# A long transformer layer on one core: its opening loads and multiplies x's first four feature tiles by token tile, and two weight loads change queue

## The chip, the cores and the metric

The kernel runs on one core of one Trainium2 chip. The metric is the device time of one execution in microseconds (us). The kernel before has a median of 1103.39 us in 3 runs (1103.22 to 1104.03). One execution was also profiled.

## The reference

The reference is one layer on x of 256 tokens by 2048 features, all in float32:

```python
h = rms_norm(x, attn_norm)
p = h @ w_in                      # 2048 x 6152: q, k, v of two groups of 8 heads, forget gates
out_a = forgetting_attention(...) # softmax with a cumulative forget bias
out_b = stick_breaking_attention(...)
x = x + concat(rms_norm(out_a), rms_norm(out_b)) @ w_out
h = rms_norm(x, ffn_norm)
u = causal depthwise conv of width 3 over h @ w_up, plus conv_b
x = x + (silu(gate) * val) @ w_down
```

Only the first steps matter here: the norm's weight on x, and the first 512 columns of the product with w_in (the queries of four heads). The division by the root mean square is a factor of each token and is applied to the finished product.

## The kernel before

**How products are made.** TensorE works in a fast 32-bit format with fewer bits of mantissa, called F32R here, so each factor is split into a high part (a copy into F32R) and a low part (the rest), and each product is three: high by high, low of x by high of w, high of x by low of w. The x side is `hT`: 16 feature tiles of 128 features (k = 0 to 15), each with a high and a low part for 256 tokens, which are two token tiles of 128 (t = 0, 1). The w side is `w_hi` and `w_lo`.

**The work as a whole.** After the opening comes the rest of the projections, the heads of both groups, the output projection and the feed-forward network. Each loads weights on SyncE's queue (SP below), copies the high part on ScalarE (`split`, line 207), subtracts for the low part on VectorE (line 208), and multiplies on TensorE (lines 229, 254, 260 and 1053).

**The opening** (`opening`, lines 385 to 474) makes `acc_q0`, 256 tokens by 512 columns. It goes through the 16 feature tiles in 8 steps c of two tiles each. Its order on TensorE, VectorE, ScalarE and SP is the order in which the code is written (a manual schedule, line 476), so an instruction that waits holds back everything behind it on its engine. The parts:

- `load_x(k, n)` (line 90) brings n feature tiles of x for both token tiles, on SP's queue. `load_w(c, which)` (line 391) brings the 512 columns of w_in for the two feature tiles of step c, or for one of them, on the queue that it is given. A half step of w is 256 KB, and so are two feature tiles of x.
- The norm's weight, 8 KB, is loaded into `prow` on ScalarE's queue (line 434) and transposed by `columns` (line 126) into `ga`, one column for each feature tile. Line 435 loads ScalarE's function table.
- `keep_busy(n)` (line 379) is n multiplications of zeros into an idle PSUM tile.
- `transposed_split(k, ga, n)` (line 133) transposes n feature tiles of x, for both token tiles, into a PSUM tile `ps_x`, one TensorE instruction for each 128 by 128 square (line 138). ScalarE then writes the high part, scaled by `ga` (line 143), and VectorE the low part (line 146). `ps_x` comes from a pool `psb` of two buffers: a third set of transposes waits until the first buffer has been read for the last time.
- `split_w(c)` (line 402) makes the high and low part of w for step c. In steps 0 and 1 most of the high parts are made on VectorE (lines 409 and 415), later all on ScalarE (line 418). The low parts are made on VectorE (line 419).
- `multiply(c, i, n, high)` (line 423) is the products of a step, line 428: both token tiles, first all that use `w_hi`, then all that use `w_lo`. A step has 12 matmuls of 512 columns, the opening 96.
- `sums_of_squares` (line 151) squares 512 features of one token tile on ScalarE, for the norm's factor, which is needed after the opening.

The first eight loads in their order on the two queues, 256 KB each but for the norm's weight:

```
ScalarE  prow (8 KB)    table load     w, tile k=1      w, tile k=2
SP       x, tiles 0, 1  w, tile k=0    x, tiles 2, 3    w, tile k=3    x, tiles 4, 5 ...
```

From the ninth load on, a load is issued when the one eight places ahead of it, counted over both queues, has landed. The products of step 0 are 8 matmuls with `w_hi` for k = 0 and 1, then four transposes (tiles 2 and 3), then 4 matmuls with `w_lo`. Then come the four transposes of tiles 4 and 5, then step 1, and so on: the transposes of step c + 1 stand ahead of the products of step c.

Of the kernel before, what the change touches and what calls it, by code (L numbers as in the profile page):

```python
# [45 lines left out]
def hybrid_layer(  # L46
# [19 lines left out]
    nc = tc.nc  # L66
    act, dve = nc.scalar, nc.vector
    xf = x.rearrange("b s d -> (b s) d")
# [18 lines left out]
    xt = [x2[:, t, :] for t in range(NT)]  # L87
    xp = xf.rearrange("(t p) d -> p t d", p=P)

    def load_x(k, n):  # L90
        nc.sync.dma_start(x2[:, :, k * P : (k + n) * P], xp[:, :, k * P : (k + n) * P])

    ident = cs[:, C_ID : C_ID + P]
# [27 lines left out]
    ga = const.tile([P, KT], F32, name="ga")  # L121
# [9 lines left out]
    hT = big.tile([P, KT, 2, S], F32R, name="hT")  # L131

    def transposed_split(k, g, n=2):

        ps = psb.tile([P, 2, S], F32, name="ps_x", tag="t")
        for j in range(n):
            for t in range(NT):
                nc.tensor.transpose(  # L138
                    ps[:, j, t * P : (t + 1) * P], xt[t][:, (k + j) * P : (k + j + 1) * P], ident
                )  # L140
        for j in range(n):
            i = k + j
            act.activation(hT[:, i, 0, :], ps[:, j, :], AF.Identity, scale=g[:, i : i + 1])
        for j in range(n):
            i = k + j
            dve.scalar_tensor_tensor(
                hT[:, i, 1, :], ps[:, j, :], g[:, i : i + 1], f32(hT[:, i, 0, :]),
                op0=ALU.mult, op1=ALU.subtract,
            )

    def sums_of_squares(ss, c, tiles=range(NT)):

        for t in tiles:
            junk = late.tile([P, 512], F32, name="junk", tag="raw", bufs=4)
            act.activation(junk, xt[t][:, c * 512 : (c + 1) * 512], AF.Square, accum_out=ss[:, t, c : c + 1])
# [78 lines left out]
    def of_half(h, part, t):  # L234
        return h[:, part, t * P : (t + 1) * P]
# [51 lines left out]
    with ExitStack() as actx:  # L287
# [91 lines left out]
        def keep_busy(n):  # L379
            for _ in range(n):  # L380
                nc.tensor.matmul(idle, zeros[:, :P], zeros, start=True, stop=True)

        ss1 = const.tile([P, NT, 4], F32, name="ss1")

        def opening():

            acc = psa.tile([P, NT, 512], F32, name="acc", tag="acc")
            pairs = [[(0, 1), (1, 1)]] + [[(0, 2)]] * 7
            raws, parts = [], []

            def load_w(c, which=None, queue=nc.sync):

                if c == len(raws):
                    raw = wraw.tile([P, 2048], F32, name="w_raw", tag="w_raw")
                    raws.extend([raw[:, :1024], raw[:, 1024:]])
                for i, n in [(which, 1)] if which is not None else [(0, 2)]:
                    queue.dma_start(
                        raws[c][:, i * 512 : (i + n) * 512].rearrange("p (a b) -> p a b", a=n),
                        rows_of(wi, 2 * c + i, n, 0, 512),
                    )  # L400

            def split_w(c):
                hi = whi.tile([P, 2048], F32R, name="w_hi", tag="w_hi")
                lo = wlo.tile([P, 2048], F32R, name="w_lo", tag="w_lo")
                parts.append([t[:, :1024].rearrange("p (a b) -> p a b", a=2) for t in (hi, lo)])
                for i, n in pairs[c]:
                    cols = slice(i * 512, (i + n) * 512)
                    if c == i == 0:
                        dve.tensor_copy(hi[:, cols], raws[c][:, cols])
                        for k in range(2):  # L410
                            transposed_split(k, ga, 1)
                    elif c == 1:
                        for j in range(2):
                            half = slice(512 * j, 512 * (j + 1))
                            dve.tensor_copy(hi[:, half], raws[c][:, half])
                        transposed_split(2, ga)
                    else:
                        act.copy(hi[:, cols], raws[c][:, cols])
                    dve.tensor_tensor(
                        lo[:, cols], raws[c][:, cols], f32(hi[:, cols]), op=ALU.subtract  # L420
                    )

            def multiply(c, i, n, high):
                hi, lo = (p[:, i : i + n] for p in parts[c])
                order = [(j, l, hi) for j in range(n) for l in range(2)] if high else [(j, 0, lo) for j in range(n)]
                for m, (j, l, r) in enumerate(order):
                    for t in range(NT):
                        nc.tensor.matmul(  # L428
                            acc[:, t, :], of_half(hT[:, 2 * c + i + j], l, t), r[:, j, :],
                            start=high and c == i == m == 0, stop=not high and c == 7 and m == n - 1,  # L430
                        )

            load_x(0, 2)
            nc.scalar.dma_start(prow[:KT, :], attn_norm[0].rearrange("(n p) -> n p", p=P))
            act.preload_act_table_set("natural_log_exp_and_others")
# [18 lines left out]
            def behind(c):  # L454
                if c:
                    transposed_split(2 * c + 2, ga)
                split_w(c + 1)

            multiply(0, 0, 1, True)
            multiply(0, 1, 1, True)  # L460
            behind(0)
            sums_of_squares(ss1, 0, [0])
            multiply(0, 0, 1, False)
            multiply(0, 1, 1, False)
            for c in range(1, 8):
                if c < 7:
                    behind(c)
                sums_of_squares(ss1, c // 2, [c % 2])
                if c == 2:
                    load_w(6)  # L470
                    load_w(7)
                multiply(c, 0, 2, True)
                multiply(c, 0, 2, False)
            return acc

        with tc.high_priority(offset=AHEAD), tc.manual_schedule(
# [698 lines left out]
```

## Time and profile before

| what | value |
|---|---|
| median of 3 runs | 1103.39 us |
| lowest, highest | 1103.22, 1104.03 us |
| the profiled execution's own time | 1103.81 us |
| its span, first to last instruction | 1102.0 us |
| granted TensorE clock, mean | 1.000 |
| bytes read from HBM | 242.82 MB |

The profiled execution took 1.8 us more than its span, and 0.42 us more than the median of the runs. PE is TensorE's matmul side, PEld its weight loads, DVE is VectorE, ACT is ScalarE, POOL is GpSimd, SP is SyncE; ACTq and SPq are the instructions with which these two issue DMAs. L428 is line 428 of the kernel. In a view in order of time, the first number is the start and the second the duration, both in us, and a group "x4" is four instructions in a row; where idle time came ahead, a bracket names it and what ended it.

### The profile page before, as it was taken

How to read it: one execution, taken by the hardware profiler on the slowest of the kernel's cores; microseconds unless marked ns; L12 is line 12 of the kernel's file. 1: busy time of each engine (PE TensorE's matmuls, PEld its weight loads, DVE VectorE, ACT ScalarE, POOL GpSimd, SP SyncE). 2: the span in 40 equal slices, each digit the busy share in tenths (PEclk: the TensorE clock that was granted, in tenths of full speed). 3: DMA queues.
4: the chain of work that ended last, by engine and by line, in shares of the span. 5: the costliest groups of instructions: out<-in, count | busy, mean ns of one | idle time of the engine just before them, and what ended most of it. 6: DMA issues, size and time to landing. Idle time of an engine off the chain costs nothing.

```text
span 1102.0 us, 14826 instructions
## 1 busy us (share of the span) xinstructions
PE 1096.5 (99%) x5868; PEld 951.2 (86%) x5868; DVE 877.7 (80%) x941; ACT 701.9 (64%) x879; POOL 44.4 (4%) x46
## 2 busy tenths in 40 slices
PE   9999999999999999999999999999999999999998
PEld 7998888888888888888888888888888888888887
DVE  5655777975775677689889988889798889889896
ACT  6544556664653566677767776767676777677753
POOL 0000000000000000000000010100000010100010
PEclk9999999999999999999999999999999999999999
DMA  8776654576545396558989597986979689997985
GB/s 288 171 244 230 188 156 153 153 231 197 184 161 186 112 317 196 181 191 209 288 223 312 191 234 264 261 269 177 315 209 303 217 218 282 241 266 198 322 208 177
DMA packets 179407, 245.89 MB, mean 223 GB/s; under 512 B 4432, under 2 KB 119018, under 8 KB 179082
## 3 DMA queue, kind: packets, MB, share of 16 engines
q1 hardware_dynamic: 162458, 209.67, 58.6%
q0 software_dynamic: 16560, 34.75, 16.8%
q8 instruction: 46, 0.75, 0.3%
q10 hardware_dynamic: 320, 0.53, 0.1%
q14 instruction: 23, 0.19, 0.0%
HBM read 242.82 MB, written 2.11 MB: 222 GB/s over the span
## 4 chain that ended last, share of the span: by engine, by line
PE 99%; DMA 0%; DVE 0%; SPq 0%; issue 0%
PE pu L254 34%; PE acc L229 22%; PE pu L260 18%; PE bank_a L229 10%; PE bank_b L229 5%; PE bank_c L229 2%; PE acc L428 2%; PE acc L1053 1%; PE ps_x L138 1%; PE ps_o L593 1%; PE bank_a L1053 1%; PE ps_p L607 0%; DMA w_raw<-in_w_in_dram 0%; PE ps_o L594 0%; PE ps_h L307 0%; PE ps_s L522 0%
## 5 line engine op out<-in xcount | busy, mean ns | idle before, releaser
L208 DVE TENSOR_TENSOR w_lo<-w_raw,w_hi 128x2048 fp32r<-128x2048 f32 (+1 forms) x196 | 439.6, 2246 | 129.5 <-ACT w_hi L207 128.6
L207 ACT CAST w_hi<-w_raw 128x2048 fp32r<-128x2048 f32 (+1 forms) x196 | 367.3, 1877 | 235.9 <-PE acc L229 66.6
L254 PE MATMUL pu<-hT,w_hi 128*128 128x512 f32 x1664 | 394.0, 390 | 0.0
L254 PEld LDWEIGHTS pu<-hT,w_hi 128*128 128x128 f32 x1664 | 310.3, 188 | 63.2
L260 PEld LDWEIGHTS pu<-hT,w_lo 128*128 128x128 f32 x1664 | 211.9, 191 | 7.0
L260 PE MATMUL pu<-hT,w_lo 128*128 128x256 f32 x1664 | 215.1, 283 | 0.0
L229 PE MATMUL acc<-w_hi,hT 128*128 128x512 f32 (+1 forms) x576 | 124.5, 368 | 0.0
L229 PEld LDWEIGHTS acc<-w_hi,hT 128*128 128x128 f32 x576 | 101.5, 188 | 14.3
L207 ACT CAST w_hi<-w_sum 128x2048 fp32r<-128x2048 f32 x30 | 57.3, 1909 | 44.2 <-PE pu L254 36.6
L208 DVE TENSOR_TENSOR w_lo<-w_sum,w_hi 128x2048 fp32r<-128x2048 f32 x30 | 68.7, 2290 | 20.8 <-ACT w_hi L207 20.7
L870 ACT ACTIVATE tap<-up,ccol 128x256 f32<-128x256 f32 x176 | 74.6, 495 | 0.0
L229 PE MATMUL acc<-w_lo,hT 128*128 128x512 f32 (+1 forms) x288 | 64.6, 366 | 0.0
L229 PEld LDWEIGHTS acc<-w_lo,hT 128*128 128x128 f32 x288 | 51.6, 188 | 7.5
L975 POOL DMA_DIRECT2D w_sum<-in_w_down_dram x20 | 25.7, 1284 | 797.7 <-DVE w_lo L208 786.1
L229 PE MATMUL acc<-w_hi,oT 128*128 128x512 f32 x192 | 46.0, 392 | 0.0
L229 PEld LDWEIGHTS acc<-w_hi,oT 128*128 128x128 f32 x192 | 35.7, 188 | 7.3
L229 PE MATMUL bank_a<-w_hi,g 128*128 128x512 f32 x160 | 40.0, 392 | 0.0
L229 PE MATMUL bank_b<-w_hi,s 128*128 128x512 f32 x160 | 40.0, 392 | 0.0
L229 PE MATMUL bank_a<-w_hi,s 128*128 128x512 f32 x160 | 40.0, 392 | 0.0
L229 PEld LDWEIGHTS bank_b<-w_hi,s 128*128 128x128 f32 x160 | 28.9, 189 | 5.2
L229 PEld LDWEIGHTS bank_a<-w_hi,g 128*128 128x128 f32 x160 | 28.8, 189 | 5.3
L229 PEld LDWEIGHTS bank_a<-w_hi,s 128*128 128x128 f32 x160 | 28.9, 189 | 5.2
(211 smaller groups left out, 1068.7 us busy)
## 6 DMA issues: line engine op xcount, KB each, us to landing
w_raw<-in_w_up_dram SPq DMA_DIRECT2D x88, 1024.0 KB, 7.5
w_raw<-in_w_down_dram SPq DMA_DIRECT2D x44, 1024.0 KB, 6.4
w_raw<-in_w_in_dram SPq DMA_DIRECT2D x36, 1024.0 KB, 5.4
w_sum<-in_w_down_dram POOLq DMA_DIRECT2D x20, 1024.0 KB, 9.9
w_raw<-in_w_out_dram SPq DMA_DIRECT2D x16, 1024.0 KB, 5.1
w_raw<-in_w_down_dram POOLq DMA_DIRECT2D x10, 1024.0 KB, 14.9
w_raw<-in_w_in_dram SPq DMA_DIRECT2D x12, 688.0 KB, 4.2
w_raw<-in_w_in_dram SPq DMA_DIRECT2D x6, 512.0 KB, 6.8
```

Source lines behind the costliest of these rows:

```text
L138: nc.tensor.transpose(ps[:, j, t * P : (t + 1) * P], xt[t][:, (k + j) * P : (k + j + 1) * P], ident)
L207: act.copy(hi[:, :n], raw[:, :n])
L208: dve.tensor_tensor(lo[:, :n], raw[:, :n], f32(hi[:, :n]), op=ALU.subtract)
L229: nc.tensor.matmul(o, lhs(i, l, t), r[:, i, :], start=starts and j == 0, stop=stops and j == 3 * n - 1, skip_group_check=more,)
L254: nc.tensor.matmul(acc[:, j, :], hi[:, i, j * P : (j + 1) * P], hT[:, k].rearrange("p a b -> p (a b)"), start=k == 0, stop=low_first and k ...
L260: nc.tensor.matmul(acc[:, j, S:], lo[:, i, j * P : (j + 1) * P], hT[:, k, 0, :], start=False, stop=not low_first and k == KT - 1,)
L428: nc.tensor.matmul(acc[:, t, :], of_half(hT[:, 2 * c + i + j], l, t), r[:, j, :], start=high and c == i == m == 0, stop=not high and c == ...
L593: nc.tensor.matmul(po, v[j][:, hs], wp[:, k], start=i == 0, stop=False)
L870: act.activation(taps[w][:, j, :], u[:, j, w : w + S], AF.Copy, scale=ccol[:, w, f : f + 1])
L975: nc.gpsimd.dma_start(mem[into][:, : nk * 512].rearrange("p (a b) -> p a b", a=nk), src, accum_op=ALU.add)
L1053: nc.tensor.matmul(o, of_half(g, l, t), r[:, i, c0 : c0 + cols], start=kh == 0 and j == 0, stop=kh == n - 1 and j == 11,)
```

## The change

It touches `opening` alone.

1. The first four feature tiles of x are loaded by token tile: two loads of 128 rows by 512 features, 256 KB each, on SP's queue, in place of `load_x(0, 2)` and `load_x(2, 2)`. The next four come in one load of 512 KB.
2. The weights of k = 0 and k = 1 both go on ScalarE's queue behind the norm's weight, and the table load stands behind these three. The weights of k = 2 and 3 go on SP's queue behind the two loads of x.
3. The four tiles of token tile 0 are transposed together into one `ps_x` (`a`), later those of token tile 1 into another (`b`). Step 0 is multiplied one feature tile and one token tile at a time, high, low of w, low of x: (k, t) = (0, 0), the transposes of token tile 1, (1, 0), (0, 1), (1, 1).
4. High and low parts of x for tiles 0 to 3 are made 128 tokens at a time. The high part of w for k = 0 stays on VectorE; those for k = 1, 2 and 3 are made on ScalarE, where k = 2 and 3 were on VectorE before.
5. The zeros' multiplications go from 14 and 4 to 12, 2 and 3. The sum of squares of token tile 0's first 512 features moves from step 0 to step 4.

The new code, cut:

```diff
+            def load_tile(t):
+                nc.sync.dma_start(xt[t][:, : 4 * P], xf[t * P : (t + 1) * P, : 4 * P])
...
+            def transposed_tile(t):
+                ps = psb.tile([P, 4, P], F32, name="ps_x", tag="t")
+                for k in range(4):
+                    nc.tensor.transpose(ps[:, k, :], xt[t][:, k * P : (k + 1) * P], ident)
+                return ps
...
+            def multiply_one(k, t):
+                hi, lo = (s[:, k % 2, :] for s in parts[k // 2])
+                for m, (l, r) in enumerate(((0, hi), (0, lo), (1, hi))):
+                    nc.tensor.matmul(
+                        acc[:, t, :], of_half(hT[:, k], l, t), r, start=k == m == 0, stop=False
+                    )
...
-            load_x(0, 2)
             nc.scalar.dma_start(prow[:KT, :], attn_norm[0].rearrange("(n p) -> n p", p=P))
+            load_tile(0)
+            load_w(0, 0, nc.scalar)
+            load_tile(1)
+            load_w(0, 1, nc.scalar)
+            load_w(1, 0)
+            load_w(1, 1)
             act.preload_act_table_set("natural_log_exp_and_others")
-            load_w(0, 0)
-            load_w(0, 1, nc.scalar)
-            load_x(2, 2)
-            load_w(1, 0, nc.scalar)
-            load_w(1, 1)
-            load_x(4, 2)
+            load_x(4, 4)
             load_w(2)
-            load_x(6, 2)
             load_w(3)
...
-            keep_busy(14)
+            keep_busy(12)
             columns(ga, prow[:KT, :], KT)
-            split_w(0)
-            keep_busy(4)
+            keep_busy(2)
+            a = transposed_tile(0)
+            keep_busy(3)
+            part_tiles(0)
+            high_part(0, 0, 1, dve.tensor_copy)
+            high_x(a, 0, 0)
+            high_x(a, 0, 1)
+            low_part(0, 0, 1)
+            low_x(a, 0, 0)
+            multiply_one(0, 0)
+            b = transposed_tile(1)
+            high_part(0, 1, 1, act.copy)
+            low_x(a, 0, 1)
+            low_part(0, 1, 1)
+            multiply_one(1, 0)
+            for k in range(2):
+                high_x(b, 1, k)
+                low_x(b, 1, k)
+            multiply_one(0, 1)
+            multiply_one(1, 1)
+            part_tiles(1)
+            for i in range(2):
+                high_x(a, 0, 2 + i)
+                high_part(1, i, 1, act.copy)
+                high_x(b, 1, 2 + i)
+                low_x(a, 0, 2 + i)
+                low_part(1, i, 1)
+                low_x(b, 1, 2 + i)
```

`high_part` copies w's high part on the engine that it is given and `low_part` subtracts on VectorE; `high_x(ps, t, k)` is ScalarE's scaled copy of 128 tokens and `low_x` VectorE's rest. From step 1 on the loop is as before, with the transposes of tiles 4 and 5 ahead of step 1's products.

More of the change, by code (lines that the diff above doesn't have):

```diff
@@ L426, in multiply @@
+            def multiply(c, high):
+                hi, lo = parts[c]
+                order = [(j, l, hi) for j in range(2) for l in range(2)] if high else [(j, 0, lo) for j in range(2)]
                 for m, (j, l, r) in enumerate(order):
@@ L471, in opening @@
                     load_w(7)
-                multiply(c, 0, 2, True)
-                multiply(c, 0, 2, False)
+                multiply(c, True)
+                multiply(c, False)
             return acc
```

62 lines of the change are left out of this document (28 added, 34 removed).

## The prediction

> **What bounds the kernel now.** I read the page first, then a view of the engines' busy time by stretches, then the chain of waits and the instructions in order of time for the opening.
>
> ```profile
> span 1102.0 us, 14826 instructions
> PE 1096.5 (99%) x5868; PEld 951.2 (86%) x5868; DVE 877.7 (80%) x941; ACT 701.9 (64%) x879; POOL 44.4 (4%) x46
> ```
>
> ```profile
> 0.00:6.50 6.50, 4.29 (x23) 2.87 (x23) 0.82 (x4) 2.38 (x4) 1.09 (x8) 1.00 0.68 195
> 6.50:9.80 3.30, 3.21 (x16) 2.70 (x17) 2.61 (x6) 1.03 (x3) 0.00 (x0) 1.00 1.04 366
> 9.80:32.00 22.20, 22.20 (x109) 17.96 (x108) 16.23 (x25) 17.37 (x37) 0.00 (x0) 1.00 0.75 258
> 32.00:560.00 528.00, 528.00 (x2873) 462.01 (x2873) 385.62 (x493) 312.32 (x440) 8.40 (x11) 1.00 0.64 198
> ```
>
> In the second fence each row has the stretch, its length, the busy time (and count) of PE, PEld, DVE, ACT and POOL, the granted clock, the DMA engines' busy share and GB/s. TensorE is busy for all of the 22.20 us from 9.80 on and all of the 528.00 us behind them. There is nothing to hide a delay in and nothing that would swallow a gain: what the opening gains or loses on TensorE before it becomes dense reaches the end in full. So the whole question is one number, the time at which TensorE reaches the first instruction from which both kernels do the same work without a gap. I take the transposes of tiles 4 and 5, at 9.87 us in the kernel before. Both kernels have behind it the same matmuls and transposes, and ahead of it the same 12 products of step 0.
>
> ```profile
> 0.73 0.46 ACTq L434 DMA_DIRECT2D prow<-in_attn_norm_dram  x1
> 0.74 0.43 SPq L91 DMA_DIRECT2D x<-in_x_dram  x1
> 1.22 1.28 ACT L435 ACT_TABLE_LOAD   x1 [1.22 <-PEq L1160]
> 1.23 0.46 SPq L397 DMA_DIRECT2D w_raw<-in_w_in_dram  x1
> 1.25 0.94 ACTq L397 DMA_DIRECT2D w_raw<-in_w_in_dram  x2
> ...
> 4.45 0.66 PE L138 MATMUL ps_x<-cs,x 128*128 128x128 f32 x4 [0.20 <-DMA x<-in_x_dram]
> ...
> 4.93 0.84 ACT L143 ACTIVATE hT<-ps_x,ga 128x256 fp32r<-128x256 f32 x2 [2.42 <-PE ps_x L138]
> ...
> 6.02 0.43 DVE L409 CAST w_hi<-w_raw 128x512 fp32r<-128x512 f32 x1 [1.56 <-DMA w_raw<-in_w_in_dram]
> 6.24 0.62 ACT L418 CAST w_hi<-w_raw 128x512 fp32r<-128x512 f32 x1 [0.48 <-DMA w_raw<-in_w_in_dram]
> 6.37 0.87 DVE L146 SCALAR_TENSOR_TENSOR hT<-ps_x,ga,hT 128x256 fp32r<-128x256 f32 x2
> ...
> 6.59 2.06 PE L428 MATMUL acc<-w_hi,hT 128*128 128x512 f32 x8 [1.05 <-DVE w_hi L409]
> 7.15 1.28 DVE L419 TENSOR_TENSOR w_lo<-w_raw,w_hi 128x512 fp32r<-128x512 f32 x2
> ...
> 8.50 0.60 PE L138 MATMUL ps_x<-cs,x 128*128 128x128 f32 x4
> ...
> 8.85 1.18 PE L428 MATMUL acc<-w_lo,hT 128*128 128x512 f32 x4
> ...
> 9.87 0.60 PE L138 MATMUL ps_x<-cs,x 128*128 128x128 f32 x4
> ```
>
> These are the opening's instructions in order of time. What starts the products is the weight of k = 0, not x: x's first tiles are there at 4.45, and the weight, issued on SP at 1.23, ends VectorE's wait at 6.02. Its copy of 0.43 us and 0.14 us to the matmul give 6.59. From there TensorE has work that is ready: eight matmuls with `w_hi` (8.50 - 6.59, some 0.23 us each with the switch) while VectorE and ScalarE make what follows. The weight of k = 1, first of the two on ScalarE's queue, issued at 1.25, ends a wait at 6.24.
>
> **The change part by part.** No matmul and no transpose is added or removed. Hidden ahead of the first product are four transposes in both kernels; four more stand between the products of step 0 in both. The zeros (one fewer) run while TensorE has nothing else. So the sum is of waits alone.
>
> *The loads.* The weight of k = 0 now is ScalarE's second DMA. It is issued when the prow DMA ends, at 1.25 instead of 1.23: no earlier. It takes the very place that k = 1's weight has before, behind prow on that queue, and beside it SP's queue again carries 256 KB of x and 256 KB more. The nearest row is 6.24, and I take it. The weight of k = 1 then takes the place of ScalarE's third DMA, for which a view of the DMA issues at that moment has the landing:
>
> ```profile
> w_raw<-in_w_in_dram ACTq DMA_DIRECT2D x1, 256.0 KB, 5.9
> ```
>
> It is issued at 1.72 (half of the 0.94 us behind 1.25), so 1.72 + 5.9 = 7.62; before, k = 1 landed at 6.24. Token tile 1 of x takes the place of SP's second load, 6.02. The queues' shares of what moved from 2 to 3 us (first fence) and from 4 to 5 us (second) are
>
> ```profile
> q1 hardware_dynamic: 199, 0.20, 76.2%
> q10 hardware_dynamic: 29, 0.01, 5.3%
> ```
>
> ```profile
> q10 hardware_dynamic: 107, 0.19, 54.7%
> q1 hardware_dynamic: 90, 0.13, 50.4%
> ```
>
> with packets, MB and share; q1 is SP's and q10 ScalarE's. ScalarE's moved 0.01 MB in the first, and took its share only later. [...]
>
> *Step 0 tile by tile.* Durations that the trace doesn't have are those of 128 columns. For ScalarE they lie between half of a 256-column copy (0.84 / 2 / 2 = 0.21) and all of it (0.42); I take 0.30. For VectorE's rest they lie between 0.22 and 0.44 (0.87 / 2); I take 0.28. A 512-column subtraction is 0.64 (1.28 / 2), a 512-column copy 0.43 on VectorE and 0.62 on ScalarE; from an engine's end to TensorE I take 0.14 as above.
>
> 1. k = 0 lands at 6.24, the copy ends at 6.67, the first matmul starts at 6.81.
> 2. The second needs `w_lo` and the third the low part of x, both from VectorE behind that copy: 6.67 + 0.64 + 0.28 = 7.59, third matmul at 7.73, TensorE free at 7.96. From 6.59 on it did six matmuls in this time before ((7.96 - 6.59) / 0.23); here three. The new wait holds the whole queue, the transposes of token tile 1 among it.
> 3. Those four transposes take 0.35 (8.85 - 8.50): 8.31. What waits for them is ScalarE's copies for t = 1.
> 4. (1, 0) needs k = 1's weight: 7.62, copy on ScalarE to 8.24, first matmul 8.38, `w_lo` to 8.88, second matmul 9.02, free behind the third at 9.48.
> 5. Six more matmuls, 0.23 each, with all that they need at hand (ScalarE's two copies of 0.30 end by 8.9, VectorE's rests by 9.5): 10.86.
> 6. The transposes of tiles 4 and 5 also need the first `ps_x` back: it is read for the last time by VectorE's rest of tile 3. Behind 8.24 ScalarE makes three copies of 128 columns (9.14), `w_hi` of k = 2 (9.76); VectorE its `w_lo` (10.40) and two rests (10.96). With 0.14 that is 11.10.
>
> So the point comes at 11.10 instead of 9.87, 1.2 us later. Instructions of one engine that don't wait overlap a little (6.02 + 0.43 is 6.45, the next starts at 6.37: 0.08), which over the last chain's few neighbours is some 0.2. I take **1.0 us later**.
>
> *Behind it.* ScalarE gets the moved sum of squares, in step 4:
>
> ```profile
> 15.41 0.64 ACT L155 ACTIVATE junk<-x 128x512 f32<-128x512 f32 x1
> 15.94 0.20 ACT L155 ACTIVATION_READ_ACCUMULATOR junk<-x 128x1 f32 x1
> 16.94 0.47 ACT L143 ACTIVATE hT<-ps_x,ga 128x256 fp32r<-128x256 f32 x1 [0.81 <-PE ps_x L138]
> ```
>
> 0.64 + 0.20 = 0.84 lie in the 0.81 in which it idles in each step; cost nothing, and without that cover at most 0.84 once. The DMA order behind the first six loads is as before but for x's tiles 4 to 7 in one load; up to and with step 2's weights it is 2.62 MB, and by the stretches 195 GB/s for 6.5 us and 366 GB/s for 3.3 us have moved 2.48 MB by 9.8. Those weights are needed when ScalarE has copied tiles 4 and 5, past 12. Cost nothing.
>
> The sum: 1103.8 (the profiled execution, span 1102.0 and 1.8 around it) + 1.0 = 1104.8; that execution stood 0.4 over the median, so the forecast is **1104.4 us**.
>
> **The rivals.**
>
> *ScalarE's weights come early.* Before, the table load (1.22, 1.28 us) stands ahead of ScalarE's weight DMAs; now behind. If it held them back, k = 0 would land after as long a time as x's first load: issued at 0.74, there at 4.45, so 3.7, hence 1.25 + 3.7 = 4.95, and k = 1 after the 4.8 of SP's weight (6.02 - 1.23), at 6.5. For it: 0.01 MB on q10 from 2 to 3 us, though issued by 1.72. Against it: the DMA issue is recorded at 1.25, inside the table load. Then (1, 0) starts by 6.5 + 0.62 + 0.14 = 7.26, its second matmul at 7.9, TensorE is free at 9.74, and the buffer comes back at 7.12 + 2.86 = 9.98: +0.1, less 0.2 of overlap, and down to -0.8 if both weights come 0.7 earlier still. I price it at -0.3: 1103.1 us. Even here step 6's chain, not the first matmul, sets the gain.
>
> *The clock is lost.* This one ends slower beyond doubt. The zeros of the start show two speeds:
>
> ```profile
> 1.06 3.04 PE L381 MATMUL idle<-zeros 128*128 128x256 bf16 x14 [1.06 <-DVE zeros L371]
> ...
> 4.95 0.60 PE L381 MATMUL idle<-zeros 128*128 128x256 bf16 x4
> ```
>
> 14 in 3.04 us, 0.22 each, and later 4 in 0.60, the last ones 0.11 apart (0.60 less the 0.27 of the last, by three). The fast speed came after some 3 us of dense work. The change has fewer zeros ahead of prow and more gaps between 6.8 and 10. If it runs three of those us at half speed, some nine matmuls and four transposes take 9 x 0.23 + 0.35 = 2.4 us more, of which the waits swallow some 0.9: +1.5, in all +2.5, 1105.9 us. It decides from 1.2 us of lost clock on top of the forecast. Against it: in the kernel before TensorE idles from 5.5 to 6.59 and loses nothing. [...]
>
> *It does not do what it says.* If the tile-by-tile order meets its data as early as before but no earlier, the wait of step 2 and that of step 4 fall into each other and the point stays near 9.9: 1103.4 us. It is the upper end of the first rival, and I count it there.
>
> **How the numbers follow.** Forecast 0.58, weights early (or no effect) 0.32, clock lost 0.10. A measurement of this kernel tells about 0.2%, 2.2 us, from no change: below 1101.2 or above 1105.6. Faster than that would need TensorE's first product some 2 us earlier and none of the new waits: 0.02, of the first rival's far end. Slower than that: most of the clock rival, and the forecast's tail with k = 1 later than 7.62 (it now shares with two SP loads of weights): 0.09. Within 0.2%: 0.89. The range takes the first rival at -0.8 (1102.6) and the forecast with k = 1 landing 1.2 later (1105.6, each us later there being a us).
>
> **What would show it.** In the profile after: VectorE's first copy of w near 6.2 (early rival: 5); ScalarE's copy of k = 1 near 7.6; between the first and second matmul of (0, 0) a wait of some 0.5 put down to VectorE's `w_lo`; the first four transposes of line 138 near 10.9, waiting for VectorE; 22 us without a gap behind them; the zeros behind prow at 0.11 us. Wrong would be a first product before 6, a stop behind the point, or granted clock below 1.00.

## The result and the profile after

| | before | after |
|---|---|---|
| median of the runs side by side | 1103.30 us (6 runs, 1103.10 to 1104.03) | 1107.39 us (6 runs, 1106.45 to 1107.77) |
| the profiled execution's own time | 1103.81 us | 1107.20 us |
| its span | 1102.0 us | 1105.4 us |
| mean granted clock | 1.000 | 0.998 |

The kernel after is slower: a ratio of 1.0035 with a 95% interval of 1.0022 to 1.0048, some 4 us. The forecast was 1104.4 us in a range that ended at 1105.6, most of its chance on no change that can be measured, and 0.09 above 1105.6. It had the direction, with a quarter of the size; and one of its own signs of being wrong came, a granted clock below 1.00.

The page of the kernel after, the two lines to set beside those of before:

```profile
span 1105.4 us, 14829 instructions
PE 1098.6 (99%) x5867; PEld 952.5 (86%) x5867; DVE 878.2 (79%) x944; ACT 703.5 (64%) x885; POOL 44.4 (4%) x46
```

The span has grown by 3.4 us and TensorE's busy time by 2.1, with one instruction fewer. So some of its instructions take longer: the four transposes of token tile 1 have 1.06 us, four transposes before 0.60. The engines' busy time by stretches, of the kernel after, with the columns of the prediction's second fence (behind the five engines come the granted clock, the DMA engines' busy share and GB/s):

```profile
0.00:6.50 6.50, 4.35 (x22) 2.89 (x22) 0.34 (x2) 1.91 (x3) 1.09 (x8) 1.00 0.62 181
6.50:9.80 3.30, 2.21 (x8) 1.67 (x8) 2.33 (x5) 0.62 (x1) 0.00 (x0) 0.79 1.05 398
9.80:14.00 4.20, 3.96 (x16) 3.00 (x16) 3.03 (x8) 3.02 (x9) 0.00 (x0) 0.76 1.04 388
14.00:18.00 4.00, 4.00 (x21) 3.29 (x20) 2.19 (x4) 3.22 (x8) 0.00 (x0) 1.00 1.05 385
32.00:560.00 528.00, 528.00 (x2866) 461.69 (x2866) 385.01 (x494) 313.27 (x444) 8.41 (x11) 1.00 0.63 198
```

From 14 us on TensorE is dense, as it was from 9.8 on before. From 6.5 to 9.8 it has 8 instructions where it had 16, and the clock granted is 0.79 from 6.5 to 9.8 and 0.76 from 9.8 to 14. So the loss lies where the prediction looked for it, ahead of the transposes of tiles 4 and 5, and it arrives in full: these start at 13.16 instead of 9.87, 3.29 later, and the span is 3.4 longer.

The instructions of the kernel after in order of time:

```profile
1.18 0.92 ACTq L396 DMA_DIRECT2D w_raw<-in_w_in_dram  x2
...
6.85 0.43 DVE L410 CAST w_hi<-w_raw 128x512 fp32r<-128x512 f32 x1 [2.15 <-DMA w_raw<-in_w_in_dram]
...
7.43 0.47 PE L444 MATMUL acc<-w_hi,hT 128*128 128x512 f32 x1 [1.58 <-DVE w_hi L410]
...
8.06 0.52 PE L444 MATMUL acc<-w_lo,hT 128*128 128x512 f32 x1 [0.16 <-DVE w_lo L417]
8.41 0.65 PE L444 MATMUL acc<-w_hi,hT 128*128 128x512 f32 x1
8.44 0.62 ACT L410 CAST w_hi<-w_raw 128x512 fp32r<-128x512 f32 x1 [2.25 <-DMA w_raw<-in_w_in_dram]
8.85 1.06 PE L427 MATMUL ps_x<-cs,x 128*128 128x128 f32 x4
...
10.73 0.62 ACT L431 ACTIVATE hT<-ps_x,ga 128x128 fp32r<-128x128 f32 x2 [0.42 <-DVE hT L436]
11.13 0.61 DVE L436 SCALAR_TENSOR_TENSOR hT<-ps_x,ga,hT 128x128 fp32r<-128x128 f32 x2 [0.43 <-ACT hT L431]
...
13.16 0.66 PE L138 MATMUL ps_x<-cs,x 128*128 128x128 f32 x4 [0.23 <-DVE hT L436]
```

Three things differ from the forecast. The weight of k = 0 ends VectorE's wait at 6.85, not 6.24. The four transposes of token tile 1 take 1.06 us; before, four took 0.60. And ScalarE and VectorE wait for each other (the brackets 0.42 and 0.43). The 0.43 was to be expected, since VectorE's low part is made from ScalarE's high part; the 0.42 was not. The chain of waits of the kernel after shows how the last two reach the point; its columns are start, duration, and engine, tile and line:

```profile
8.06 0.99 PE acc L444 x2
9.05 0.87 PE ps_x L427 x4
...
9.95 0.38 ACT hT L431
...
10.35 0.36 DVE hT L436
...
10.73 0.62 ACT hT L431 x2
11.36 0.52 ACT w_hi L410
...
11.90 0.56 DVE w_lo L417
...
12.51 0.61 DVE hT L436 x2
...
13.16 0.66 PE ps_x L138 x4
```

From the end of the transposes of token tile 1 (9.05 + 0.87 = 9.92) to the point at 13.16 the chain doesn't touch TensorE at all. It goes through ScalarE, VectorE, ScalarE, VectorE. The second piece is a turn: ScalarE's second copy out of `b` waits until VectorE has taken the first rest out of the same `b`, though from other columns. It is the PSUM tile that they take turns on and not `hT`, which the brackets name: from 11.13 to 11.35 ScalarE copies out of `a` (the second of its two at 10.73) while VectorE takes a rest out of `b`, and both write `hT`.

The same view by stretches that are one clock window (3.41 us) long, of the kernel after and then of the kernel before:

```profile
5.01:8.43 3.42, 1.68 (x11) 1.01 (x9) 1.54 (x4) 0.63 (x2) 0.00 (x0) 1.00 1.00 367
8.43:11.84 3.41, 3.41 (x11) 2.83 (x11) 1.75 (x5) 2.10 (x6) 0.00 (x0) 0.50 1.04 392
```

```profile
3.83:7.24 3.41, 2.16 (x14) 1.50 (x13) 1.39 (x5) 1.46 (x3) 0.00 (x0) 1.00 0.99 320
```

After 3.42 us in which TensorE was busy for 1.68, 3.41 us were granted at 0.50. In the kernel before a stretch of that length with 2.16 busy is followed by none.

### The profile page after: what moved, and what is told of

It is laid out like the page before. It is cut to its first block, busy times and chain, and to the rows that moved or that the text cites. A ratio compares the mean times of both kernels' runs of the same rounds, so it can differ in the third digit from the quotient of the medians.

```text
span 1105.4 us, 14829 instructions
## 1 busy us (share of the span) xinstructions
PE 1098.6 (99%) x5867; PEld 952.5 (86%) x5867; DVE 878.2 (79%) x944; ACT 703.5 (64%) x885; POOL 44.4 (4%) x46
## 4 chain that ended last, share of the span: by engine, by line
PE 99%; DMA 1%; DVE 0%; ACT 0%; ACTq 0%; issue 0%
PE pu L254 34%; PE acc L229 22%; PE pu L260 18%; PE bank_a L229 10%; PE bank_b L229 5%; PE bank_c L229 2%; PE acc L453 2%; PE acc L1094 1%; PE ps_x L138 1%; PE ps_o L634 1%; DMA w_raw<-in_w_in_dram 1%; PE bank_a L1094 1%; PE ps_p L648 0%; PE ps_o L635 0%; PE ps_h L307 0%; PE ps_s L563 0%
```

## The experiments

Three theories stood at the start; the expectations call them by letters. **M**, mine: three things add up, the weight of k = 0 that comes late, the turns of ScalarE and VectorE on one PSUM tile, and half a clock. **K**: the clock is the whole of it. **W**: it is the waits of TensorE in the new order and for its weights, and the clock plays no part. A difference of single medians below about 1 us is inside the intervals here; such ones are read from the traces, and a trace is one execution: the four kernels with the same loads (after, e1, e8, e11) have the weight of k = 0 at 6.51 to 7.04. "The point" is the start of the transposes of tiles 4 and 5.

| kernel | what it is | k = 0 lands | first product | point | median, us | ratio to before (95%) |
|---|---|---|---|---|---|---|
| before | | 6.02 | 6.59 | 9.87 | 1103.30 to 1103.87 | 1 |
| after | | 6.85 | 7.43 | 13.16 | 1107.39 | 1.0035 (1.0022 to 1.0048) |
| e1_filled | after, zeros in the gaps | 6.76 | 7.77 | 12.76 | 1106.56 | 1.0026 (1.0016 to 1.0035) |
| e4_order | after, weights as before | 5.83 | 6.41 | 12.37 | 1106.45 | 1.0026 (1.0016 to 1.0035) |
| e8_highs | after, no turns | 7.04 | 7.62 | 12.94 | 1106.98 | 1.0030 (1.0017 to 1.0043) |
| e11_highs_filled | e1 and e8 | 6.51 | 7.14 | 11.49 | 1105.70 | 1.0017 (1.0008 to 1.0026) |
| e10_mended | e1, e4 and e8 | 6.00 | 7.38 | 11.38 | 1105.25 | 1.0012 (1.0003 to 1.0022) |
| e6_table | after, table load first | 6.60 | 7.17 | 12.91 | 1107.24 | 1.0031 (1.0020 to 1.0042) |
| e3_queues | before, weights as after | 6.01 | 6.58 | 10.91 | 1105.09 | 1.0013 (1.0004 to 1.0023) |
| e9_tiles | e3, x by token tile | 7.05 | 8.26 | 13.47 | 1106.37 | 1.0030 (1.0017 to 1.0044) |
| e2_thinned | before, fewer zeros | 6.03 | 6.60 | 9.90 | 1104.36 | 1.0009 (1.0000 to 1.0018) |
| e12_before_filled | before, more zeros | 5.91 | 6.48 | 9.78 | 1103.91 | 1.0003 (0.9994 to 1.0012) |
| e7_first | before, x on ScalarE's queue | by 7.22 | 8.24 | 12.87 | 1107.82 | 1.0036 (1.0023 to 1.0049) |
| e13_wfirst | before, weight ahead of prow | by 4.87 | 7.45 | 11.48 | 1105.95 | 1.0021 (1.0012 to 1.0030) |

**e1_filled: the gaps of the kernel after filled with zeros**, so that the clock is kept.

```diff
-            def multiply_one(k, t):
+            def multiply_one(k, t, fill=0):
                 hi, lo = (s[:, k % 2, :] for s in parts[k // 2])
                 for m, (l, r) in enumerate(((0, hi), (0, lo), (1, hi))):
+                    if m == 1:
+                        keep_busy(fill)
...
-            keep_busy(3)
+            keep_busy(15)
...
-            multiply_one(0, 0)
+            multiply_one(0, 0, 3)
...
-            multiply_one(1, 0)
+            multiply_one(1, 0, 3)
```

> The kernel after, with more multiplications of zeros on TensorE: 15 in place of 3 ahead of the first product, and 3 between the first and second matmul of the products (0, 0) and (1, 0). Nothing else changes; its loads and waits are those of the kernel after. Theory M (late weights, then a serial chain of ScalarE and VectorE, and one clock window of 3.4 us lost on top): the clock stays at full speed, the matmuls between 8.4 and 11.8 us take 0.23 us in place of 0.43, but the chain of ScalarE and VectorE holds the transposes of tiles 4 and 5 (13.16 us in the kernel after) at about 12.5, so about 0.7 us faster than the kernel after: 1106.7. Theory K (the clock is the whole of what the forecast missed): 1.7 us faster, 1105.7, transposes near 11.5. Theory W (the waits alone, the clock's loss lies inside them): no change, 1107.4.

1106.56 us, as M said. In order of time:

```profile
5.38 2.63 PE L381 MATMUL idle<-zeros 128*128 128x256 bf16 x15
7.77 0.48 PE L446 MATMUL acc<-w_hi,hT 128*128 128x512 f32 x1
...
8.90 0.60 PE L427 MATMUL ps_x<-cs,x 128*128 128x128 f32 x4
...
12.76 0.66 PE L138 MATMUL ps_x<-cs,x 128*128 128x128 f32 x4 [0.83 <-DVE hT L436]
```

The transposes take 0.60 again, so the clock was kept, and all ten runs have a mean clock of 1.000, where four of the kernel after's six have 0.998. The fifteen zeros have a price: in this execution they ran at half speed until 7.08 (the fifteen took 2.63 us; in the kernel before four later ones took 0.60) and held the first product to 7.77, though its weight was there at 6.76. And the point still waits for VectorE, and it comes 3.26 behind their end (12.76 - 8.90 - 0.60), as in the kernel after (3.24). The clock is not the whole: K falls. It is not nothing either, so W falls too.

**e2_thinned: the zeros alone**, fewer of them in the kernel before.

```diff
-            keep_busy(14)
+            keep_busy(12)
...
-            keep_busy(4)
```

> The kernel before with fewer multiplications of zeros: 12 in place of 14 at the start and none in place of 4 ahead of the first product. Its loads and its order are unchanged. [...] Theory W: the zeros do nothing, 1103.3, clock 1.000.

1104.36 us, 1103.48 to 1107.05 in 10 runs, where before on that chip had 1103.18 to 1105.59 in 31. The median hardly moves, the spread grows upward. M and K had one window at half speed, 1104.5 to 1105.0 us and a granted clock of 0.998. That the spread is the clock isn't shown: all ten runs have a mean clock of 0.999 or 1.000, so none has the lost window; a late start at half speed would not show in that column, which has 1.00 over such a stretch in e4 (see the end). The profiled execution (1104.38) has its point at 9.90, only 0.03 later than before, and a span 0.6 longer all the same. The rest comes behind 1079 us, where TensorE waits 0.25 for VectorE near 1090. So at least there the added time did not come in the opening.

**e3_queues: the weights' queues alone**, in the kernel before.

```diff
-            act.preload_act_table_set("natural_log_exp_and_others")
-            load_w(0, 0)
-            load_w(0, 1, nc.scalar)
+            load_w(0, 0, nc.scalar)
             load_x(2, 2)
-            load_w(1, 0, nc.scalar)
+            load_w(0, 1, nc.scalar)
+            load_w(1, 0)
             load_w(1, 1)
+            act.preload_act_table_set("natural_log_exp_and_others")
```

> The kernel before with the change's queues for the weights alone: k = 0 and 1 both on ScalarE's queue behind the norm's weight and ahead of the table load, k = 2 and 3 on SP's. The loads of x and the order of the products are those of the kernel before. Theory M: k = 0 lands near 6.8 us in place of 6.0 and k = 1 near 8.4 in place of 6.2, the first product starts at 7.4 in place of 6.6, the products of k = 1 wait until 9.2, and the transposes of tiles 4 and 5 come near 11.5 in place of 9.9: 1.6 us slower than before, 1104.9, or up to 1105.6 if the gap costs a clock window. Rival (the late weights come from the loads of x by token tile, not from the queue): k = 0 near 6.1, 1103.4.

```profile
6.01 0.43 DVE L409 CAST w_hi<-w_raw 128x512 fp32r<-128x512 f32 x1 [1.35 <-DMA w_raw<-in_w_in_dram]
...
7.81 0.62 ACT L418 CAST w_hi<-w_raw 128x512 fp32r<-128x512 f32 x1 [1.81 <-DMA w_raw<-in_w_in_dram]
...
8.48 1.22 PE L428 MATMUL acc<-w_hi,hT 128*128 128x512 f32 x4 [0.70 <-ACT w_hi L418]
```

Here the weight of k = 0 is as early as before (6.01; before 6.02), against M's expectation, while that of k = 1 is 1.6 later (6.24 before) and TensorE waits 0.70 for it. That makes the point 1.04 later and the median 1.5 (1105.09, with 1103.57 for before beside it). So the queue by itself does not explain the 6.85 of the kernel after. What else could hold that weight back is x, whose loads by token tile have rows of 2 KB where two feature tiles have rows of 1 KB. That became M's second form, tried in e9.

**e4_order: the order alone**, the kernel after with the weights on the queues of before.

```diff
-            load_w(0, 0, nc.scalar)
-            load_tile(1)
-            load_w(0, 1, nc.scalar)
-            load_w(1, 0)
+            load_w(0, 0)
+            load_w(0, 1, nc.scalar)
+            load_tile(1)
+            load_w(1, 0, nc.scalar)
```

> The kernel after with the weights of k = 0 to 3 on the queues that they have in the kernel before (k = 0 and 3 on SP's, 1 and 2 on ScalarE's); x by token tile, the order tile by tile and the place of the table load stay. Theory M: k = 0 lands near 6.1 and k = 1 near 6.3, the first product starts near 6.7, but the chain of 128-column copies still takes until 11.6 for the transposes of tiles 4 and 5: 1.8 us slower than before, 1105.1, some 0.7 more if a clock window is lost. Rival (the late weights are the whole loss): 1103.4.

```profile
6.41 0.77 PE L444 MATMUL acc<-w_hi,hT 128*128 128x512 f32 x1 [0.18 <-DVE w_hi L410]
...
8.06 1.05 PE L427 MATMUL ps_x<-cs,x 128*128 128x128 f32 x4
...
12.37 0.66 PE L138 MATMUL ps_x<-cs,x 128*128 128x128 f32 x4 [0.67 <-DVE hT L436]
```

The first product is earlier than in the kernel before (6.41; 6.59), and still the point is 2.50 later: 9.11 for the end of the transposes, and again 3.26 of turns behind it. In this execution the transposes also ran at half speed, and matmuls were 0.79 long until 10.08; the clock had not come up yet. From the first product to the end of the transposes it took 2.70, where e1 at full speed took 1.73 (9.50 - 7.77), so 0.97 of the 2.50 can be put down to that. The order costs most of the rest, with early weights too; the fastest of the ten runs, 1105.60, is still 2.0 above the median of before.

**e9_tiles: x by token tile**, added to e3; the products in the order of before.

```diff
-            load_x(0, 2)
+            load_tile(0)
...
-            load_x(2, 2)
+            load_tile(1)
```

> The run with the weights' queues alone (1105.1) and, in addition, the change's first two loads of x by token tile (128 rows by 512 features) in place of two by feature tiles; the order of the products is that of the kernel before. There k = 0 landed at 6.0, in the kernel after at 6.8, on the same queue. Theory M2 (x in rows of 2 KB takes a larger share of the DMA engines from ScalarE's queue than x in rows of 1 KB): k = 0 lands near 6.8 again, 0.6 to 0.8 us slower than the run with the queues alone, 1105.8. Rival (the order of the products or chance moved the landing): k = 0 near 6.0, 1105.1, or earlier products by what x gains.

```profile
6.85 0.90 PE L138 MATMUL ps_x<-cs,x 128*128 128x128 f32 x3 [2.01 <-DMA x<-in_x_dram]
...
7.05 0.43 DVE L412 CAST w_hi<-w_raw 128x512 fp32r<-128x512 f32 x1 [2.40 <-DMA w_raw<-in_w_in_dram]
...
8.62 0.62 ACT L421 CAST w_hi<-w_raw 128x512 fp32r<-128x512 f32 x1 [0.35 <-DMA w_raw<-in_w_in_dram]
```

With nothing changed but how x's first two loads are cut, the same weight on the same queue goes from 6.01 to 7.05 and k = 1's from 7.81 to 8.62. The landings of one kernel's loads differ by up to 0.53 (6.51 to 7.04), so one trace alone would say little; but all six with ScalarE's queue and x by token tile have 6.51 or later, and with x by token tile and the weight on SP's queue it is 5.83 (e4) and 6.00 (e10). So both halves of the load part are needed for the late weight: ScalarE's queue, and x in longer rows (and half as many) beside it. In the traces of before and after SP's queue moves 0.20 MB in 199 packets and 0.16 MB in 83 from 2 to 3 us, some 1.0 and 1.9 KB each, and ScalarE's queue 0.25 MB and 0.19 MB from 2 to 5 us. My guess is that longer rows on one queue leave less to the other; how they would do so isn't shown. (This kernel needs x's second load ahead of any product, so its time says nothing of the change. Its profiled execution was its slowest, 1109.91 us: of the 6.1 us more in the span 3.60 are there at the point, the rest comes behind 1065 us.)

**e8_highs: no turns.** The kernel after with both of ScalarE's copies out of a PSUM tile ahead of both of VectorE's rests, and the high parts of w for k = 2 and 3 behind those copies.

```diff
             for k in range(2):
                 high_x(b, 1, k)
+            for k in range(2):
                 low_x(b, 1, k)
...
             for i in range(2):
                 high_x(a, 0, 2 + i)
-                high_part(1, i, 1, act.copy)
+            for i in range(2):
                 high_x(b, 1, 2 + i)
+            for i in range(2):
+                high_part(1, i, 1, act.copy)
+            for i in range(2):
                 low_x(a, 0, 2 + i)
+            for i in range(2):
                 low_part(1, i, 1)
                 low_x(b, 1, 2 + i)
```

> The kernel after with the copies of x reordered so that ScalarE and VectorE do not take turns on one PSUM tile: both high parts of a pair ahead of both low parts, for token tile 1 of k = 0 and 1 and for k = 2 and 3; then the high parts of w for k = 2 and 3. Loads, products and zeros as in the kernel after. Theory M2 (3.25 us go from the end of token tile 1's transposes to the point, by a chain in which each engine waits for the other's last reading of the same PSUM tile): the chain drops to some 1.7 us, TensorE's own nine products become what is late, and the transposes of tiles 4 and 5 come 0.4 us earlier (clock lost) to 1.0 us earlier (clock kept): 1106.4 to 1107.0. Rival (the chain is the engines' own work, as the forecast summed it): no change, 1107.4.

1106.98 us, hardly less. The chain of waits, then the clock windows:

```profile
9.01 0.53 PE ps_x L427 x4
9.54 3.56 PE acc L444 x9
13.10 0.44 PE ps_x L138 x4
```

```profile
5.81:9.22 3.41, 1.79 (x11) 1.09 (x9) 2.01 (x5) 1.21 (x3) 0.00 (x0) 1.00 1.05 400
9.22:12.63 3.41, 3.41 (x11) 2.72 (x9) 2.03 (x6) 2.79 (x8) 0.00 (x0) 0.50 1.03 386
```

The turns are gone from the chain: from the transposes to the point it is TensorE alone. VectorE's last rest out of `a` now ends 1.82 behind the transposes (11.36), not 3.19. But its nine matmuls take 3.56, 0.40 each, because a window at 0.50 lies over them. The turns and the half clock lie side by side, and taking away one shows the other.

**e11_highs_filled: both cures**, the diffs of e1 and e8 together.

> The kernel after with both cures at once: zeros in the gaps (15, 3, 3) and the copies of x reordered so that the engines do not take turns on one PSUM tile; its loads unchanged, so the weight of k = 0 stays at 6.8. Theory M2: alone the cures gave 0.8 (zeros) and 0.4 us (order), since each was held by the other's cause; together the transposes of tiles 4 and 5 come near 11.8 in place of 13.2, so 1.2 to 1.4 us faster than the kernel after: 1106.1, and 0.8 us slower than the run with the weights' queues put right as well (1105.25). Rival (the two overlap): 1106.6.

```profile
8.49 0.44 PE ps_x L427 x4
8.93 0.40 PE acc L446
9.33 0.34 PE idle L381 x3
9.67 1.98 PE acc L446 x8
11.65 0.44 PE ps_x L138 x4
```

1105.36 to 1105.82 us in 10 runs, all below the fastest of the kernel after (1106.45). The point is 1.67 earlier than in the kernel after (13.16 to 11.49), with eight matmuls in 1.98, 0.25 each, and no other engine in the chain. Of the 1.67, 0.29 is a first product that came earlier (7.14; 7.43) because the weight landed at 6.51 this time. Counted from the first product to the point, the kernel after takes 5.73, e1 4.99, e8 5.32 and the two cures together 4.35: 0.74 and 0.41 alone, 1.38 together. That is little more than their sum, as was expected.

**e10_mended: the weights' queues of before as well**, the diffs of e1, e4 and e8 together.

> The change's tile-by-tile order with three things put right at once: the weights on the queues of the kernel before, the copies reordered as in the run without the turns, and zeros in the gaps (15, 3 and 3). Theory M2: first product near 6.7, nine further products of 0.23 us without a stop behind the transposes of token tile 1, the transposes of tiles 4 and 5 near 10.6, 0.7 us behind the kernel before: 1104.0. Theory W (one row of waits more or less, tile by tile is slow in itself): 1105.5 or more.

1105.25 us; I had expected 1104.0, and W 1105.5 or more. The k = 0 weight is there at 6.00, but the first product starts at 7.38:

```profile
5.41 2.21 PE idle L381 x15
7.62 0.24 PE acc L446
7.86 0.34 PE idle L381 x3
```

My own 15 zeros, at half speed until 6.46 (all of them in 2.42 us), hold it (the chain counts the matmul's 0.24 from their end). The point is 1.51 later than before: the first product 0.79 later (7.38 - 6.59), and from there to the point 4.00 instead of 3.28, of which two groups of three zeros are 2 x 0.34. Those groups were meant to fill the waits for the low parts of w, but here nothing waited for these:

```profile
6.46 0.69 DVE L417 TENSOR_TENSOR w_lo<-w_raw,w_hi 128x512 fp32r<-128x512 f32 x1
...
7.59 0.68 DVE L417 TENSOR_TENSOR w_lo<-w_raw,w_hi 128x512 fp32r<-128x512 f32 x1
```

They were there at 7.15 and 8.27, ahead of the zeros at 7.86 and 9.35 in the chain. So nearly all of the 1.51 is zeros, and the run doesn't say what the order by tiles costs in itself.

**e6_table: the table load ahead of the weights**, as in the kernel before.

```diff
             nc.scalar.dma_start(prow[:KT, :], attn_norm[0].rearrange("(n p) -> n p", p=P))
+            act.preload_act_table_set("natural_log_exp_and_others")
...
-            act.preload_act_table_set("natural_log_exp_and_others")
```

> The kernel after with ScalarE's table load back ahead of the weights' loads on its queue. First rival of the prediction (the table load holds ScalarE's DMAs back): the weights land 0.9 to 1.3 us later than in the kernel after, 7.8 and 9.4, and the time is 1108.4. Theory M2 (it does not touch the queue): k = 0 near 6.9, 1107.4.

1107.24 us, k = 0 at 6.60, k = 1 at 8.24: the place of the table load is worth nothing that can be told. Five of the six runs had a mean clock of 0.998, the sixth 1.000, and that one was the fastest, 1106.20 against 1107.00 to 1107.54. Elsewhere the column doesn't part the runs so well: the kernel after has 1106.45 and 1107.43 at 1.000, and 1107.20 to 1107.77 at 0.998; e8 has 1106.49 at 1.000 and 1106.54 at 0.998. In e3 the one run at 0.998 is 1.5 us over the slowest of the others (1106.71; 1105.18). The column doesn't count a late start at half speed, either (see the end). So what a lost window costs is not settled here; the runs allow anything from nothing to some 1.5 us.

**e12_before_filled, e7_first, e13_wfirst: could the kernel before be made faster?** More zeros behind its first transposes (12 for 4); x's first load on ScalarE's queue with prow on GpSimd's; the weight of k = 0 ahead of prow on ScalarE's queue.

```diff
-            keep_busy(4)
+            keep_busy(12)
```

> The kernel before with 12 multiplications of zeros in place of 4 ahead of the first product. [...] Theory W: 1103.6, no change in spread.

```diff
-            load_x(0, 2)
-            nc.scalar.dma_start(prow[:KT, :], attn_norm[0].rearrange("(n p) -> n p", p=P))
+            nc.scalar.dma_start(x2[:, :, : 2 * P], xp[:, :, : 2 * P])
+            nc.gpsimd.dma_start(prow[:KT, :], attn_norm[0].rearrange("(n p) -> n p", p=P))
```

> An attempt to beat the kernel before: its first load of x goes on ScalarE's queue, the norm's weight on GpSimd's, and so the weight of k = 0 is SP's first load, issued at 0.74 in place of 1.23. All else as in the kernel before. If issue time and place in the queue set the landing: k = 0 lands near 5.2, x near 5.0, the first product starts at about 6.1, 0.4 us faster than before, 1103.0. If the DMA engines' shared rate sets it: x lands so much later that the copies of x end near 6.5 and nothing is gained, 1103.5; with the norm's weight late on GpSimd's queue it could be slower, 1104.

```diff
             load_x(0, 2)
+            load_w(0, 0, nc.scalar)
             nc.scalar.dma_start(prow[:KT, :], attn_norm[0].rearrange("(n p) -> n p", p=P))
...
-            load_w(0, 0)
-            load_w(0, 1, nc.scalar)
+            load_w(0, 1)
```

> A second attempt to beat the kernel before: the weight of k = 0 is ScalarE's first load, ahead of the norm's weight, and the weight of k = 1 takes its place as SP's second load; all else as in the kernel before. If place in the queue sets the landing: k = 0 lands near 5.2 in place of 6.0 and the first product then waits for x's copies, which wait for the norm's weight behind it (near 5.3): first product at 6.1 in place of 6.6, 1103.1 beside 1103.6 for the kernel before. If x and the weight, now issued at the same time, slow each other by as much: no change, 1103.6; if the norm's weight comes only near 6, slower, 1104.

None is. e12 is the kernel before to within its interval (1103.91 us), with no run above 1104.49 where before went up to 1105.51; M had put it at 1103.5, with a few executions near 1104.7. The two others lose by the norm's 8 KB: its product on TensorE waits 2.67 us for it in e7 (to 6.89) and 1.41 in e13 (to 5.64); before, it ran at 4.03. e13 was also at half speed until 9.04 (its first eight products take 2.83, before 2.06): its first product is 0.86 later than before, its point 1.61. e7 also lost a window:

```profile
4.32:7.74 3.42, 0.85 (x6) 0.70 (x7) 0.51 (x2) 0.24 (x1) 0.00 (x0) 1.00 1.04 367
7.74:11.15 3.41, 3.41 (x12) 2.70 (x10) 2.75 (x6) 1.10 (x3) 0.00 (x0) 0.50 1.06 376
```

No kernel tried beats the one before.

## Why the prediction was wrong in size

Its frame held: all lies ahead of one point, nothing behind it hides or adds (3.29 at the point, 3.4 in the span), and the path from the transposes of token tile 1 to the point goes through ScalarE and VectorE, as step 6 had it, and ends in VectorE's rests. Three steps failed: the landing of the weights (0.62), step 3, which put the lost clock at nothing (0.93), and step 6 with its credit for overlap, which left out the turns on one PSUM tile (0.68).

The path failed too. Step 6 was counted from ScalarE's copy of k = 1's weight (7.62 + 0.62 = 8.24), with the transposes of token tile 1 ready 0.07 later, and the range took each us of that weight's delay for a us. In the kernel after that copy ends at 9.06, and ScalarE then waits 0.89 for the transposes: TensorE holds the path until 9.92. The table therefore measures step 6 from the end of the transposes, in the forecast 8.31:

| stretch | forecast | measured | more by |
|---|---|---|---|
| first product (steps "the loads" and 1) | 6.81 | 7.43 | 0.62 |
| to the third product (step 2) | 0.92 | 0.98 | 0.06 |
| to the end of token tile 1's transposes (step 3) | 0.58 | 1.51 | 0.93 |
| to the point (step 6, less the credit for overlap) | 2.56 | 3.24 | 0.68 |
| the point | 10.87 | 13.16 | 2.29 |

- **The loads, 0.62.** I took k = 1's landing of before for the same place on ScalarE's queue, 6.24, and noted that SP's queue carries 256 KB of x beside it either way. The size was the same, the rows were not: e3 with 1 KB rows has 6.01, e9 with 2 KB rows 7.05. The queue by itself made no difference to that weight: in e3 the weight is there at 6.01 on ScalarE's queue, before at 6.02 on SP's. The weight of k = 1 was 0.82 late (8.44 instead of 7.62), but it is not on the path: with it early (6.14), e4 has the same 3.26 behind the transposes.
- **Step 3, 0.93.** With the clock kept (e1) the stretch takes 0.83 (8.67 to 9.50), so 0.68 is half a clock. The other 0.25 is the length of the last transpose, which I had counted by its interval to the next. "The clock is lost" had a chance of 0.10 and the argument against it was that TensorE idles from 5.5 to 6.59 before and loses nothing. That showed that one gap is harmless, not that two more are. In the traces 3.41 us at 0.50 followed a stretch in which TensorE was busy for 1.68 of 3.42 us (e8: 1.79 of 3.41), with no gap above 1.6 (1.58 ahead of the first product; e8: 1.45). My price for the rival, 1.5 us on top, was about twice what came: 0.68 at the path, and 0.83 between the medians of the kernel after and e1.
- **Step 6 with its credit, 0.68.** I added up each engine's own work. I did not see that ScalarE and VectorE read one PSUM tile in turn, so that ScalarE's second copy stands behind VectorE's first rest: 0.36 by the chain, about half of it. The traces show that wait (ScalarE's 0.42 in the kernel after, gone from the chain in e8), not what makes it. With them at hand, code in which the two alternate can be read for it beforehand. The other half is mostly pieces of 128 columns that are longer than I took: a copy 0.37 for 0.30, a rest 0.34 to 0.35 for 0.28, 0.32 over the three copies and two rests. The credit itself was not too large: neighbours on one engine overlap by 0.08 to 0.11, 0.38 in all between 9.92 and 13.16, and the 3.24 has that in it.
- **Right:** the second product waits for VectorE's `w_lo` (8.06, 0.63 behind the first); the moved sum of squares and the DMAs behind the opening cost nothing (TensorE has 4.00 of 4.00 from 14 us on); "weights come early" is refuted (e6); the first product does not move forward.
- **The chances.** Forecast and clock rival were priced as alternatives. They add. Undone one at a time the causes gave little at the point, 0.40 for e1, 0.79 for e4 and 0.22 for e8, but each of these traces has something else that came late: zeros that hold the first product (e1), a clock that is up only at 10.08 (e4), a weight that lands 0.19 later (e8). Counted from the first product the zeros are worth 0.74, the order of the copies 0.41, both 1.38.

What stays open: what raises or keeps the clock (below), and what the order by tiles would cost with the clock kept and no zeros in its way; that wasn't tried.

## What to carry to other kernels

This kernel is dense behind a point, and nearly the whole of the change is the shift of that point (3.29 of 3.4 us). The path to such a point must be followed across engines with every handover, not summed by engine: cutting work into smaller pieces turned eight matmuls of cover (2.06 us before) into chains with one. Where ScalarE and VectorE read one PSUM tile, writing all reads of the one ahead of those of the other gave 0.41 us between the first product and the point (e8). Move a load to another queue only after looking at the row length of what runs beside it (k = 0 at 6.01 with rows of 1 KB in e3, at 7.05 with 2 KB in e9), and before thinning out what fills TensorE's gaps count its busy share over windows of 3.4 us as well as its longest gap (in these traces half speed followed 1.79 us busy or less, and not some 2.0 or more).

## What the runs showed of the hardware

- The clock: once it had been up, half speed came as 3.41 us at 0.50, with edges that differ from trace to trace (8.43 to 11.84 in the kernel after, 9.22 to 12.63 in e8, 7.74 to 11.15 in e7), and the mean clock of the same code was 0.998 in some runs and 1.000 in others (the kernel after: 0.998 in four of six). Counted in such windows from the first raise on, those with TensorE busy for 0.85 (e7), 1.63 (e6), 1.68 (after) and 1.79 us (e8) were followed by half speed, those with some 2.0 or more (e2, whose edge its trace leaves open), 2.16 (before) and 2.58 or more (e1, e3, e4) were not. The longest idle stretch in them parts them in the same way, 1.45 or more against 1.43 or less, so these traces can't tell a share from a gap. What raises the clock is less plain: full speed followed 2.77 us busy of 3.42 in one trace (before, to 3.83), and did not follow 3.10 of 3.42 in another (e4, to 6.67, one window ahead of its raise at 10.08).
- The granted clock of the views doesn't count the start at half speed. The last fence, of e4 by stretches, has 1.00 where ten instructions of TensorE, six products and four transposes, fill 3.41 us:

```profile
6.67:10.08 3.41, 3.41 (x10) 2.56 (x10) 1.78 (x5) 0.60 (x3) 0.00 (x0) 1.00 1.02 371
```

  Ahead of the first raise, the length of a matmul (0.79 there, 0.40 later in the same trace) tells the clock; the column doesn't.
- An 8 KB load was there for TensorE by 4.03 and 4.24 us first on ScalarE's queue (before, after), at 5.64 behind 256 KB on that queue (e13), and at 6.89 on GpSimd's (e7): the same size, and by its place up to 2.9 us later.
